# A larger first chunk in tile 0, so that its store and the load of tile 2 are issued later, in a streaming SiLU-multiply kernel

## The chip, the cores and the metric

The kernel runs on one core of a Trainium2 chip. The metric is the time of one execution in microseconds of the device. I quote medians of the fast runs, with the granted clock at 1.00. "Span" is the length of the one profiled execution; it is some 2 us shorter than the device time of the same execution.

## The reference

```python
# x: float32, (32, 512, 2048), random normal
x1, x2 = x[..., :1024], x[..., 1024:]
out = x1 * (1 / (1 + np.exp(-x1))) * x2        # float32, (32, 512, 1024)
```

134.2 MB are read and 67.1 MB written, 201.3 MB in all. There is one activation (SiLU) and one multiply for each output element.

## The kernel before

The 16,384 rows are cut into 16 tiles of 128 partitions x 8 rows. There are two input buffers and two output buffers. Loads are issued on ScalarE's DMA queue and stores on SyncE's. Each tile is computed in four chunks of 2 rows, SiLU on ScalarE and then the multiply on VectorE. After the last chunk the whole tile (4 MB) is stored, and the load of the tile after next (8 MB) is issued. Only the last tile is stored chunk by chunk.

```python
    K = 8
    KC = 2
    PLAN = [K] * (num_rows // (P * K))
    in_pool = ctx.enter_context(tc.tile_pool(name="in_pool", bufs=2))
    out_pool = ctx.enter_context(tc.tile_pool(name="out_pool", bufs=2))
    # ... cut: plan, view(), the first load moved ahead of the start barrier ...
    def load(i):
        xt = in_pool.tile([P, K, in_cols], dt, name="xt")
        nc.scalar.dma_start(out=xt[:, :plan[i][1], :], in_=view(x_flat, i))
        loaded[i] = xt

    load(0)
    load(1)
    for i in range(n_tiles):
        # ... cut: k, xt, last, ov ...
        ot = out_pool.tile([P, K, half], dt, name="ot")
        for c in range(0, k, KC):
            ce = min(c + KC, k)
            nc.scalar.activation(out=ot[:, c:ce, :], in_=xt[:, c:ce, :half],
                                 func=mybir.ActivationFunctionType.Silu)
            nc.vector.tensor_mul(out=ot[:, c:ce, :], in0=ot[:, c:ce, :],
                                 in1=xt[:, c:ce, half:])
            if last:
                nc.sync.dma_start(out=ov[:, c:ce, :], in_=ot[:, c:ce, :])
        if not last:
            nc.sync.dma_start(out=ov, in_=ot[:, :k, :])
        if i + 2 < n_tiles:
            load(i + 2)
```

## Time and profile before

| | before |
|---|---|
| median, first 3 runs | 470.96 us (470.91 to 471.08) |
| span of the profiled run | 468.9 us |
| VectorE / ScalarE busy | 30% / 25% |
| rate over the span | 429 GB/s |

These are lines of the page of the kernel before: its span, the busy tenths of the DMA engines in 40 equal slices, the chain that ended last, and the DMA issues with their time to landing.

```profile
span 468.9 us, 269 instructions
...
DMA  9899999999999998999999999999999989999998
...
DMA 80%; DVE 15%; ACT 3%; DVEq 0%; issue 0%
DMA xt<-in_x_dram 80%; DVE ot L92 15%; ACT ot L87 3%; DVEq L128 0%
...
out_dram<-ot SPq DMA_DIRECT2D x15, 4096.0 KB, 39.8
out_dram<-ot SPq DMA_DIRECT2D x4, 1024.0 KB, 5.7
xt<-in_x_dram ACTq DMA_DIRECT2D x16, 47.1
```

The DMA line has no slice under 8 tenths. The two compute engines are idle most of the time, so their work can cost time only if it leaves the DMA engines without work. The chain names VectorE for 15% of the span. That is a trap: a chain follows who released whom, and a load is released by the multiply that frees its buffer. Whether the engines stood empty meanwhile is another question, and the DMA line says no.

These are the groups of instructions of the kernel before (busy us, then the mean ns of one, then idle time and who ended it).

```profile
L92 DVE TENSOR_TENSOR ot<-ot,xt 128x2048 f32<-128x2048 f32 x64 | 142.3, 2286 | 319.5 <-ACT ot L87 319.5
L87 ACT ACTIVATE ot<-xt 128x2048 f32<-128x2048 f32 x64 | 116.9, 1897 | 338.8 <-DMA xt<-in_x_dram 338.8
```

This is the timeline of the kernel before around tiles 0 and 1 (start us, duration us, engine, line, operation, count). A row of a queue, SPq or ACTq, is the issuing of a DMA, not its transfer; the first SPq row merges four issues.

```profile
21.88 7.31 ACT L87 ACTIVATE ot<-xt 128x2048 f32<-128x2048 f32 x4 [19.31 <-DMA xt<-in_x_dram]
23.82 8.90 DVE L92 TENSOR_TENSOR ot<-ot,xt 128x2048 f32<-128x2048 f32 x4 [23.82 <-ACT ot L87]
32.74 81.08 SPq L100 DMA_DIRECT2D out_dram<-ot  x4
32.75 0.35 ACTq L74 DMA_DIRECT2D xt<-in_x_dram  x1
44.54 7.31 ACT L87 ACTIVATE ot<-xt 128x2048 f32<-128x2048 f32 x4 [15.36 <-DMA xt<-in_x_dram]
...
55.41 0.37 ACTq L74 DMA_DIRECT2D xt<-in_x_dram  x1
```

Store 0 and load 2 are issued at 32.7 us, load 1 lands at 44.5 us. And this is its end:

```profile
451.03 7.31 ACT L87 ACTIVATE ot<-xt 128x2048 f32<-128x2048 f32 x4 [21.57 <-DMA xt<-in_x_dram]
452.97 8.90 DVE L92 TENSOR_TENSOR ot<-ot,xt 128x2048 f32<-128x2048 f32 x4 [19.98 <-ACT ot L87]
455.29 6.94 SPq L98 DMA_DIRECT2D out_dram<-ot  x4
```

The trace also holds one record for every DMA packet: queue, size, start, duration. I summed them over steps of 5 us. These are not lines of a view, but my own sums for the kernel before, in GB/s:

```
  from us   loads  stores    sum      (counted from the first load packet, at 1.14 us of the span)
        0     363       0    363
        5     434       0    434
      ...
       30     424       0    424
       35     261     105    366
       40     224     210    433
      ...     the sum is 431 to 434 in every step up to 450
      450       0     434    434
      455       0     428    428
      460       0     428    428
      465       0      79     79      (the last packet ends)
```

But for the start, one dip at 35 to 40 us and the last stores, all 16 engines work at their full rate throughout. 201.3 MB at 434 GB/s is 464 us of the 468.9 us span. This agrees with the Trainium skill, "DMA: Bandwidth & Descriptors", section "Where 436 GB/s comes from", which gives a ceiling of 435.2 GB/s.

The packets of one engine show the rest. I followed each engine by joining the end of a packet to the start of the next (the records carry no engine number). The packet times here and below are counted from a zero that lies 0.13 us before that of the timelines: take 0.13 us off to compare the two. This is one of the 16 chains, L for a 64 KB load packet, s for a 32 KB store packet, as start+duration in us:

```
before, one engine:  L33.39+2.44 L35.83+3.18 s39.01+1.21 L40.22+2.42 s42.63+1.21 s43.85+1.21 L45.06+2.42 s47.47+1.21
```

A load packet takes 2.42 us and a store packet 1.21 us, in turn, for the rest of the run. Where two stores follow each other, as at 42.63 us, a 4-byte record of the load queue takes the turn between them: each DMA ends with one such record on every engine, and below an engine has "finished" a load when this record has gone out. One packet is long: the load packet just ahead of the first store packet took 3.18 us. It was so on all 16 engines, 0.87 us lost on average (0.76 to 1.00), and it does not come again. I call it the entry round.

### The profile page before, as it was taken

How to read it: one execution, taken by the hardware profiler on the slowest of the kernel's cores; microseconds unless marked ns; L12 is line 12 of the kernel's file. 1: busy time of each engine (PE TensorE's matmuls, PEld its weight loads, DVE VectorE, ACT ScalarE, POOL GpSimd, SP SyncE). 2: the span in 40 equal slices, each digit the busy share in tenths (PEclk: the TensorE clock that was granted, in tenths of full speed). 3: DMA queues.
4: the chain of work that ended last, by engine and by line, in shares of the span. 5: the costliest groups of instructions: out<-in, count | busy, mean ns of one | idle time of the engine just before them, and what ended most of it. 6: DMA issues, size and time to landing. Idle time of an engine off the chain costs nothing.

```text
span 468.9 us, 269 instructions
## 1 busy us (share of the span) xinstructions
DVE 142.3 (30%) x64; ACT 118.2 (25%) x65; POOL 0.2 (0%) x4
## 2 busy tenths in 40 slices
DVE  0070705106061160601507025070250702407034
ACT  1142406023060330603206032060420604106051
POOL 0000000000000000000000000000000000000000
DMA  9899999999999998999999999999999989999998
GB/s 431 375 447 403 447 447 447 403 419 431 447 447 403 447 492 363 442 492 391 458 403 439 456 447 403 409 442 447 447 403 444 467 386 447 442 419 481 400 409 354
DMA packets 5042, 201.35 MB, mean 429 GB/s; under 512 B 560, under 2 KB 560, under 8 KB 560
## 3 DMA queue, kind: packets, MB, share of 16 engines
q10 hardware_dynamic: 2304, 134.22, 66.4%
q1 hardware_dynamic: 2736, 67.11, 33.2%
q14 instruction: 2, 0.02, 0.0%
HBM read 134.22 MB, written 67.11 MB: 429 GB/s over the span
## 4 chain that ended last, share of the span: by engine, by line
DMA 80%; DVE 15%; ACT 3%; DVEq 0%; issue 0%
DMA xt<-in_x_dram 80%; DVE ot L92 15%; ACT ot L87 3%; DVEq L128 0%
## 5 line engine op out<-in xcount | busy, mean ns | idle before, releaser
L92 DVE TENSOR_TENSOR ot<-ot,xt 128x2048 f32<-128x2048 f32 x64 | 142.3, 2286 | 319.5 <-ACT ot L87 319.5
L87 ACT ACTIVATE ot<-xt 128x2048 f32<-128x2048 f32 x64 | 116.9, 1897 | 338.8 <-DMA xt<-in_x_dram 338.8
L87 ACT ACT_TABLE_LOAD x1 | 1.3, 1283 | 1.3 <-PEq L117 1.3
L117 POOL MEMSET const-uint8-127<- 128x1 uint8 x1 | 0.1, 102 | 0.0
L117 POOL MEMSET const-bfloat16-1.0<- 128x1 bf16 x1 | 0.1, 101 | 0.0
L117 POOL MEMSET const-float32-0.0<- 128x1 f32 x1 | 0.1, 98 | 0.2 <-issue 0.2
L117 POOL MEMSET const-float32-1.0<- 128x1 f32 x1 | 0.1, 98 | 0.0
## 6 DMA issues: line engine op xcount, KB each, us to landing
out_dram<-ot SPq DMA_DIRECT2D x15, 4096.0 KB, 39.8
out_dram<-ot SPq DMA_DIRECT2D x4, 1024.0 KB, 5.7
xt<-in_x_dram ACTq DMA_DIRECT2D x16, 47.1
```

Source lines behind the costliest of these rows:

```text
L87: nc.scalar.activation(out=ot[:, c:ce, :], in_=xt[:, c:ce, :half], func=mybir.ActivationFunctionType.Silu,)
L92: nc.vector.tensor_mul(out=ot[:, c:ce, :], in0=ot[:, c:ce, :], in1=xt[:, c:ce, half:],)
L117: nc = _bacc.Bacc("TRN2", target_bir_lowering=False, num_devices=1)
```

## The change

Its intent is to shift the moment at which the first store and the third load meet the load in flight, by giving tile 0 one large chunk first.

```diff
+    CHUNKS_FIRST = [4, 2, 2]
...
-        for c in range(0, k, KC):
-            ce = min(c + KC, k)
+        c = 0
+        for kc in CHUNKS_FIRST if i == 0 else [KC] * (k // KC):
+            ce = c + kc
             nc.scalar.activation(
...
+            c = ce
         if not last:
```

No DMA is added, removed or reordered.

## The prediction

> **What bounds the kernel.** The 16 DMA engines, from the first microsecond to the last. The page's slices show DMA at 0.9 or more in 39 of 40 slices, while DVE is busy 30% and ACT 25%. I summed the trace's packet records over 5 us steps: 434 GB/s in every step from 5 us on but for two losses. The first-load packets take 3.0 to 3.4 us instead of 2.42 us (about 0.8 us lost). The load packets that start at 35.8 us, just after the first store is issued, take 3.2 to 3.4 us instead of 2.42 us (about 0.85 us lost, once, on all 16 engines). 201.3 MB at 434 GB/s is 464 us of the 468.9 us span. The rate agrees with the 435 GB/s ceiling in the Trainium skill, "DMA: Bandwidth & Descriptors", section "Where 436 GB/s comes from".
>
> The chain of waits (DMA 80%, DVE 15%) names a load, then ACT 1.9 us, then four multiplies, then the next load. Its DVE part is no lost time: load i+1 and older stores keep the engines full meanwhile.
>
> **What the change does.** Bytes, buffers, DMA count and DMA order are unchanged. In tile 0 alone two 128x2048 pairs become one 128x4096 pair. One 128x2048 activation takes 1.89 us and one multiply 2.28 us (groups of instructions). With the small fixed part of each paid once, I estimate 3.6 us and 4.4 us for the large ones. The first multiply starts at 25.5 us instead of 23.8 us, and tile 0 ends at about 34.5 us instead of 32.7 us. Store 0 and load 2 are issued some 1.7 us later.
>
> **How much is on the critical path.** Almost none. At 34.5 us load 1 still has two or three 64 KB packets for every engine, so no engine runs dry. The packets alternate afterwards, one load of 2.42 us and one store of 1.21 us (the skill, same page, section "Queues, rings and completion order", says that engines go round-robin between queues by packet; this trace agrees). The new issue time lies close to a packet boundary (35.8 to 36.15 us). Either the store still goes in at 39 us and nothing shifts, or it goes in one load packet later, about 41.4 us. Then load 1 lands about 1.2 us earlier (43.3 instead of 44.5 us), each later tile starts about 1.2 us earlier, and that much more store backlog is left at the end. Load 15 then lands at about 449.8 instead of 451.0 us, followed by about 19 instead of 17.8 us of stores. The end is the same, since bytes and rate are. The last store chunk, issued at 461.9 us, started only at 464.5 us, so the tail has slack.
>
> **Prediction.** 470.9 us, range 470.1 to 472.0 us. Faster by over 2%: 0.01; within 2%: 0.97; slower by over 2%: 0.02.
>
> **What would show it.** Right: tile 0 has a 3.6 us activation and a 4.4 us multiply, its store is issued at 34.5 us, DMA stays full in every slice, one slow round of load packets remains, and the span is within 1 us. Wrong: a slice with a DMA gap near 35 to 45 us, packets longer than 2.42 / 1.21 us afterwards, or ACT waiting for a store instead of a load.
>
> **What would make it wrong.** If the store enters at different rounds on different engines, reads and writes would mix in time; now all engines change together within 0.4 us. Should mixed packets be slower, the whole run slows. Or the one-time loss of 0.85 us vanishes or doubles.

## The result, and the profile after

| | before | after |
|---|---|---|
| median | 471.02 us (470.71 to 471.44, 6 runs) | 471.44 us (471.0 to 471.99, 6 runs) |
| ratio of fast runs, 95% interval | | 1.0009 (0.9997 to 1.0022) |
| span of the profiled run | 468.9 us | 469.9 us |

A ratio is the mean time of one kernel's fast runs over that of the other's of the same rounds, so it is not quite the ratio of the medians. The range, 470.1 to 472.0 us, holds the median.

These are the same lines of the page, now of the changed kernel:

```profile
span 469.9 us, 267 instructions
...
DMA  9899999999999999999999999999999999999987
...
DMA 80%; DVE 15%; ACT 3%; DVEq 0%; issue 0%
DMA xt<-in_x_dram 80%; DVE ot L94 15%; ACT ot L89 3%; DVEq L131 0%
...
out_dram<-ot SPq DMA_DIRECT2D x15, 4096.0 KB, 41.3
out_dram<-ot SPq DMA_DIRECT2D x4, 1024.0 KB, 5.9
xt<-in_x_dram ACTq DMA_DIRECT2D x16, 47.1
```

No gap opened in the DMA line (its last slice, where the stores run out, reads 7 instead of 8), and the chain has the same shares. Stores take 41.3 us to land instead of 39.8 us. These are its groups of instructions, which hold 62 small and one large instruction each:

```profile
L94 DVE TENSOR_TENSOR ot<-ot,xt 128x2048 f32<-128x2048 f32 (+1 forms) x63 | 142.3, 2320 | 320.4 <-ACT ot L89 320.4
L89 ACT ACTIVATE ot<-xt 128x2048 f32<-128x2048 f32 (+1 forms) x63 | 116.9, 1925 | 339.7 <-DMA xt<-in_x_dram 339.7
```

Busy time is what it was. The durations by tile give 3.62 us for the large activation and 4.43 us for the large multiply (3.6 and 4.4 us were estimated). This is the changed kernel's timeline at the start and at the end:

```profile
21.87 7.22 ACT L89 ACTIVATE ot<-xt 128x4096 f32<-128x4096 f32 x3 [19.29 <-DMA xt<-in_x_dram]
25.52 8.83 DVE L94 TENSOR_TENSOR ot<-ot,xt 128x4096 f32<-128x4096 f32 x3 [25.52 <-ACT ot L89]
34.38 51.68 SPq L103 DMA_DIRECT2D out_dram<-ot  x3
34.38 0.35 ACTq L75 DMA_DIRECT2D xt<-in_x_dram  x1
45.85 7.31 ACT L89 ACTIVATE ot<-xt 128x2048 f32<-128x2048 f32 x4 [16.76 <-DMA xt<-in_x_dram]
...
56.73 0.37 ACTq L75 DMA_DIRECT2D xt<-in_x_dram  x1
```

```profile
451.85 7.31 ACT L89 ACTIVATE ot<-xt 128x2048 f32<-128x2048 f32 x4 [21.68 <-DMA xt<-in_x_dram]
453.80 8.89 DVE L94 TENSOR_TENSOR ot<-ot,xt 128x2048 f32<-128x2048 f32 x4 [20.09 <-ACT ot L89]
456.12 6.94 SPq L100 DMA_DIRECT2D out_dram<-ot  x4
```

The issue comes 1.64 us later (34.38 instead of 32.74 us), as forecast. But load 1 lands at 45.8 us, 1.3 us later than before, where I had expected it earlier or unchanged. The packets say why (my own chains again):

```
after, one of 15 engines:   L33.43+2.43 L35.86+2.42 L38.28+3.41 s41.68+1.21 s42.90+1.21 L44.11+2.42
after, the 16th engine:     L33.67+2.42 L36.09+2.94 s39.02+1.21 L40.23+4.18 s44.41+1.21 s45.63+1.21 L46.84+2.42
```

On 15 engines the store entered one load packet later than before, at 41.7 to 42.2 us, and the packet ahead of it lost 1.0 to 1.6 us instead of 0.87 us. The 16th engine took the store a round earlier, at 39.0 us, and then lost again, 2.29 us in all. It finished load 1 at 45.6 us, the others between 42.9 and 43.5 us. (In every later load, up to load 15, the last engine's record comes 2.4 us after the median one.) The skill, "DMA: Bandwidth & Descriptors", section "Why a DMA increments its semaphore by 16 and not by 1", says that the engines of a DMA finish independently and that only the full count of 16 means that all data has landed. This trace agrees: ScalarE started tile 1 at 45.85 us, after the sixteenth. From there on all packets last 2.42 or 1.21 us again but for isolated losses of about 0.3 us on single engines, which the kernel before has too. The last packets of 14 engines end between 467.2 and 467.8 us, the last of all at 468.7 us.

### The profile page after: what moved, and what is told of

It reads as the page before. It is cut to its first block, busy times and chain, and to the rows that moved or that the text cites. A ratio compares the mean times of both kernels' runs of the same rounds, so it can differ in the third digit from the quotient of the medians.

```text
span 469.9 us, 267 instructions
## 1 busy us (share of the span) xinstructions
DVE 142.3 (30%) x63; ACT 118.1 (25%) x64; POOL 0.2 (0%) x4
## 3 DMA queue, kind: packets, MB, share of 16 engines
q1 hardware_dynamic: 2736, 67.11, 33.1%
## 4 chain that ended last, share of the span: by engine, by line
DMA 80%; DVE 15%; ACT 3%; DVEq 0%; issue 0%
DMA xt<-in_x_dram 80%; DVE ot L94 15%; ACT ot L89 3%; DVEq L131 0%
## 5 line engine op out<-in xcount | busy, mean ns | idle before, releaser
L94 DVE TENSOR_TENSOR ot<-ot,xt 128x2048 f32<-128x2048 f32 (+1 forms) x63 | 142.3, 2320 | 320.4 <-ACT ot L89 320.4
L89 ACT ACTIVATE ot<-xt 128x2048 f32<-128x2048 f32 (+1 forms) x63 | 116.9, 1925 | 339.7 <-DMA xt<-in_x_dram 339.7
## 6 DMA issues: line engine op xcount, KB each, us to landing
out_dram<-ot SPq DMA_DIRECT2D x15, 4096.0 KB, 41.3
```

## The experiments

The theories of the first question, whether the delay costs time:

- A: the delay is absorbed, because load 1 still has packets queued; time is lost only where an engine has nothing to do.
- B: the chain of waits is the cost, so 1.6 us of delay cost 1.6 us.
- C: it is the larger instructions that matter, not the delay.

The second question is where the last +0.4 us come from: from the entry round (G), or from noise (N).

### after_again: the changed kernel on the chip of the next three runs

No edit. 

> The changed kernel once more, on the same chip as the next three runs. Theory A (the delay is absorbed by the queued packets of load 1; what is left of the difference is the dead time of the slowest of the 16 DMA engines in the one slow round of packets when the store queue starts): 0 to +1.0 us against the kernel before, and the run differs from it by what its slowest engine loses in that round. Rival B (the chain of waits is the cost: each us by which tile 0's store and load 2 come later is a us of the run, here 1.6 us): +1.6 us.

Measured: 471.58 us against 471.05 us before, ratio 1.0015 (1.0001 to 1.0029). In this profile no engine was a round apart (41.7 to 42.5 us), the mean loss in the entry round was 1.24 us, and the span was 469.6 us. B is refuted by the size.

### e4_delay_2: the delay of the store alone

```diff
+    spare = spare_pool.tile([P, 1, in_cols], dt, name="spare")    # set to 1.0 at the start
...
         # tile 0 keeps its four chunks of 2 rows
+        if i == 0:
+            for _ in range(2):
+                nc.vector.tensor_mul(out=ot[:, k-1:k, :650], in0=ot[:, k-1:k, :650],
+                                     in1=spare[:, :, :650])
         if not last:
             nc.sync.dma_start(out=ov, in_=ot[:, :k, :])
```

> The kernel before with all its 2-row chunks, and two short extra multiplies by one in tile 0 that delay its store and load 2 by about 1.7 us: the delay alone, without the 4-row instructions. Issue near 34.4 us as in the changed kernel. Theory A: within 1 us of the kernel before and within 0.5 us of the changed kernel, the store entering at a later round of packets, about 41.5 us. Rival B: +1.6 us. Rival C (the larger instructions themselves matter): equal to the kernel before, unlike the changed one.

Measured: 471.58 us, ratio 1.0008 (0.9995 to 1.0020), the same median as the changed kernel beside it. The store was issued at 34.67 us. One part of my plan was wrong: load 2 does not depend on these multiplies and was still issued at 32.9 us. So this run delays the store alone, and it looks like the changed kernel: mean loss 1.40 us in the entry round, two engines a round early, losing up to 2.5 us. Rival C is not needed: small chunks with a late store give the same picture in the packets. In the time this run alone decides nothing, as its interval holds both 1 and the changed kernel's 1.0009. Whether C adds anything below 0.5 us is not resolved by these runs.

### e2_one_chunk: tile 0 in one chunk, both issues 5 us later

```diff
-    CHUNKS_FIRST = [4, 2, 2]
+    CHUNKS_FIRST = [8]
```

> Tile 0 in one chunk of 8 rows: activation about 7.1 us, multiply about 8.7 us, so store 0 and load 2 are issued near 37.7 us, 5 us later than in the kernel before, while load 1 has packets until about 41 us. Theory A: between -0.5 and +1.0 us. Rival B: +5 us.

Measured: 470.97 us (470.71 to 471.11), ratio 0.9997 (0.9984 to 1.0009). The timeline of this run, at its start and at its end:

```profile
37.90 44.68 SPq L103 DMA_DIRECT2D out_dram<-ot  x3
37.91 0.36 ACTq L75 DMA_DIRECT2D xt<-in_x_dram  x1
42.20 7.31 ACT L89 ACTIVATE ot<-xt 128x2048 f32<-128x2048 f32 x4 [13.05 <-DMA xt<-in_x_dram]
```

```profile
448.82 7.31 ACT L89 ACTIVATE ot<-xt 128x2048 f32<-128x2048 f32 x4 [21.68 <-DMA xt<-in_x_dram]
```

A delay three times as long as that of the change costs nothing. Load 1 lands earlier, at 42.2 us, as no store packet has come ahead of its last one, and the last load lands at 448.8 instead of 451.0 us. The span is still 468.9 us, because the stores that were passed over have to be written at the end. An earlier landing of every load is worth nothing here. All engines entered together (41.4 to 42.0 us) with a mean loss of 0.82 us.

### e6_delay_18: meant to delay both by 18 us

The edit of e4_delay_2 with 15 multiplies of 1,024 columns. 

> The kernel before with 15 extra multiplies by one in tile 0: store 0 and load 2 are issued near 51 us, long after the last packet of load 1 (about 41 us). Theory A: the DMA engines are empty from about 41 to 52 us, and the run is 10 to 12 us longer, not 18. Rival B: +18 us. If the run is less than 8 us longer, the tail or another slack takes part of the gap, and theory A is incomplete.

Measured: 474.92 us, ratio 1.0063 (1.0031 to 1.0095), with three executions at 474.8 to 475.2 us and one at 471.1 us. The expectation was wrong on a false premise: again only the store was held back, to 51.8 us, while load 2, issued at 32.9 us, kept the engines full. In the profile one engine entered a round before the other 15 (56.6 us against 58.6 to 59.0 us) and lost 2.37 us there, the others 1.0 to 1.2 us. Its packets of the last load ended at 451.4 us, those of the others at 447.7 to 448.6 us, and one engine's last packet ended at 472.1 us, all others' at 468.2 to 468.3 us. The entry round is not the whole of that lag: in the chain of the early engine 21 later load packets, from 101 to 426 us, took 2.46 to 2.78 us and lost another 3.0 us in all, against at most 0.2 us on any other engine. Why this engine was slow is open. One engine that lags makes the whole core wait: the last tile had to wait for the buffer of store 13, which landed on this engine 4 us after the others (452.6 us), and the other engines stood empty for up to 0.9 us before the last stores. I had no profile of the execution at 471.1 us; that no engine lagged in it is a guess.

### e10_both_late_18: the mended form

```diff
+        if i == 0:
+            for _ in range(15):      # reads xt: load 2 has to wait
+                nc.vector.tensor_mul(out=spare[:, :, :1024], in0=xt[:, k-1:k, :1024],
+                                     in1=xt[:, k-1:k, half:half+1024])
+            nc.vector.tensor_scalar_mul(out=ot[:, k-1:k, :8], in0=ot[:, k-1:k, :8],
+                                        scalar1=1.0)     # writes ot: store 0 has to wait
```

> A mended form of the 18 us delay, whose first form had delayed only the store, as load 2 did not depend on the extra multiplies. Here 15 spare multiplies read tile 0's input, so that load 2 waits for them, and a tiny scaling of its output after them holds the store: both are issued near 51.5 us, while load 1's last packet ends near 41 us. Theory A: engines empty from 41 to about 52.5 us, and the run 10 to 12 us longer. Rival B: 18 us longer. If the run is under 8 us longer, theory A fails.

Measured: 483.43 us against 471.27 us, 12.2 us longer, ratio 1.027 (1.0251 to 1.0289). Both were issued at 51.7 us, 19 us late. The windows of this run around the hole (busy us of DVE, ACT and POOL, granted clock, DMA share, GB/s):

```profile
30.00:41.00 11.00, 10.79 (x9) 0.00 (x0) 0.00 (x0) 1.00 0.88 381
41.00:53.00 12.00, 10.41 (x10) 0.90 (x1) 0.00 (x0) 1.00 0.26 71
53.00:80.00 27.00, 8.90 (x4) 6.41 (x4) 0.00 (x0) 1.00 0.97 415
```

(The middle line is not quite zero, as the first packets of load 2 start just before 53 us.) By the packets every engine is empty from 40.5 to 41.1 us until 52.8 to 53.8 us, about 12 us, and about 12 us is what the run loses. At this dose the delay costs, and it costs what the engines stand empty: A holds, B (18 us) does not. No dose between 5 and 19 us was run, so where the cost begins is not measured.

### e11_load_late_2: load 2 alone 1.7 us later

```diff
+        if i == 0:
+            for _ in range(2):       # after the store's issue; reads xt only
+                nc.vector.tensor_mul(out=spare[:, :, :650], in0=xt[:, k-1:k, :650],
+                                     in1=xt[:, k-1:k, half:half+650])
         if i + 2 < n_tiles:
             load(i + 2)
```

> Load 2 alone comes 1.7 us later (two spare multiplies that read tile 0's input after the last real one); store 0 stays at 32.8 us. If the store's time of issue alone sets what the slow round costs, this equals the kernel before within 0.3 us: store packets enter at 39 us on all engines and load 1 lands near 44.5 us. If load 2's issue sets it, it looks like the changed kernel: entry near 41.5 us and +0.4 us or more.

Measured: 470.87 us against 471.27 us, ratio 0.9992 (0.9978 to 1.0005).

```profile
33.06 52.32 SPq L102 DMA_DIRECT2D out_dram<-ot  x3
34.74 0.33 ACTq L76 DMA_DIRECT2D xt<-in_x_dram  x1
45.17 7.31 ACT L89 ACTIVATE ot<-xt 128x2048 f32<-128x2048 f32 x4 [15.67 <-DMA xt<-in_x_dram]
```

The later load by itself does nothing. Entry at 39.1 to 39.9 us on all engines, mean loss 0.85 us, as in the kernel before. Of the two issues that the change moves, the store's is the one that alters the entry round.

### e7_warm_before: is the slow round the first use of the store queue?

```diff
     load(0)
     load(1)
+    warm = warm_pool.tile([P, 1, 128], dt, name="warm")
+    nc.sync.dma_start(out=warm, in_=view(x_flat, 0)[:, :1, :128])
```

> The kernel before, with one extra small load (128 x 128 elements, 64 KB) issued on the store queue at the start. It asks what makes the one slow round of load packets just ahead of the first store packets (35.8 us in the kernel before, 0.85 us lost). Theory F (first use of the queue): the slow round is gone from 35.8 us, and the run is 0.5 to 0.9 us shorter, unless the loss only moves to the small load at the start. Theory I (an idle queue that gets work again): the slow round stays at 35.8 us, as the queue has been idle for some 30 us, and the run is equal within 0.4 us or longer by the small load's 0.2 us.

Measured: 471.09 us against 471.27 us, ratio 1.0000 (0.9988 to 1.0013). The slow round stayed: load packets from 35.8 us on took 3.1 to 3.4 us, mean loss 0.84 us. So it is not the first use of the queue as such. The small DMA was a load, so a cost of the queue's first *write* is not excluded; it remains open beside "an idle queue that gets work".

### e9_store_first_chunk: tile 0 stored chunk by chunk

```diff
-            if last:
+            if last or i == 0:
                 nc.sync.dma_start(out=ov[:, c:ce, :], in_=ot[:, c:ce, :])
-        if not last:
+        if not last and i != 0:
             nc.sync.dma_start(out=ov, in_=ot[:, :k, :])
```

> The kernel before, with tile 0 stored chunk by chunk (four stores of 1 MB from about 26 us on) while load 2 is still issued at 32.7 us. If the slow round belongs to the store queue's start, it moves to the load packets that start near 28.6 or 31 us, with none at 35.8 us; if it belongs to load 2, it stays near 35.8 us. Theory A for the time: within 0.6 us of the kernel before, though the first store comes 6.6 us earlier and its landing too. Rival B (issue time is run time): about 6 us faster.

Measured: 475.0 us against 471.27 us, ratio 1.0082 (1.0068 to 1.0096): 3.7 us slower. Neither theory had this. The waits of this run (engine, what waited on what, total us, times, longest):

```profile
ACT ot L87 <- DMA xt<-in_x_dram: 296.8, 14, 24.4
ACT ot L87 <- DMA out_dram<-ot: 40.0, 1, 40.0
```

ScalarE waits 40.0 us, once, for a store. With chunks of 2 rows a store packet is 8 KB (0.31 us) instead of 32 KB, and it alternates one to one with a 64 KB load packet. In one of the 16 chains:

```
e9, one engine:  L28.58+2.42 s31.00+0.31 L31.31+2.55 s33.86+0.31 L34.16+2.45 s36.61+0.31 L36.92+2.44 s39.35+0.31
```

The skill, "DMA: Bandwidth & Descriptors", section "Queues, rings and completion order", says that an engine goes round-robin between queues at packet granularity. This trace agrees, and shows the consequence: the share of the rate follows the packet size. In my 5 us sums, from 30 to 40 us after the first packet, loads took 368 to 382 GB/s and stores 40 to 52 GB/s. Store 0 therefore landed so late that tile 2 got its output buffer only at 90.5 us, long after its load; by then both loads were done, and when the stores ran out too, all 16 engines had no packet for 2.5 to 3.1 us from 99.4 us on. The packets after this hole lost another 1.4 to 1.8 us. Together that is some 4.4 us on each engine, less 0.3 us that the earlier load packets lost less than before; the two profiled executions differ by 4.3 us (473.2 and 468.9 us), the medians by 3.7 us. Again, time is lost only where engines have nothing to do or start again. As for its first question: no load packet ahead of the first store lost more than about 0.2 us here (28.5 to 33 us), and none near 35.8 us lost 0.8 us. In the ten runs of the table below, whose first store packets are of 32 KB, that round lost 0.8 us or more on average. So the loss depends on more than the queue waking up.

### e12_one_packet, e13_third_packet: the store later by one packet, and by a third

The edit of e4_delay_2 with three multiplies of 630 columns (store at 35.4 us), or one (33.9 us); load 2 stays at 32.9 and 33.0 us.

> The kernel before with its store 0 alone delayed by one load packet, 2.4 us, to about 35.3 us (load 2 stays at 32.9 us): later than in the changed kernel. Theory G: the store meets the packets in the phase that it has in the kernel before, enters at about 41.5 us on all engines together, the load packet ahead of it loses about 0.85 us, and the run equals the kernel before within 0.3 us. If a later store simply costs more (rival L), it loses as much as the changed kernel or more: 1.2 us in that round and +0.5 us or more in the run.

Measured: 470.90 us (470.81 to 470.99) against 470.86 us, ratio 1.0000 (0.9987 to 1.0014). All engines entered together, at 41.6 to 42.3 us. The mean loss was 1.20 us, not the 0.85 us that G had said; and the run was equal all the same, which is against rival L. So a mean loss of 1.2 us, in place of 0.87 us, hardly shows in the run, though it does reach the end: the 16 engines' last packets end at 467.6 us on average, against 467.2 us in the kernel before.

> The kernel before with store 0 alone delayed by 0.8 us, to about 33.7 us, a third of a load packet. Theory G: still in the middle of a packet, so the entry stays at about 39 us on all engines, the loss is 0.85 us or less, and the run equals the kernel before within 0.3 us. Rival L: +0.2 us, half of what the changed kernel shows.

Measured: 471.10 us, ratio 1.0004 (0.9992 to 1.0017). G was wrong on the entry: ten engines entered at 39.3 to 39.8 us and six at 41.8 to 42.0 us. The mean loss was 1.37 us but evenly spread, 1.67 us at most, and the last packets of all engines ended within 1.1 us.

### after_third: a third profile of the changed kernel

No edit. 

> The changed kernel a third time, for a third profile and chip. Theory G (what is left of the difference, +0.4 to +0.5 us, comes from the round in which the store queue starts: with the store issued near 34.4 us its entry falls on a packet boundary, so that the load packet ahead of it loses 1.1 to 1.4 us on average instead of 0.85 us and single engines may be a round apart): 0.2 to 0.9 us above the kernel before, with the entry at about 41.8 us and a mean loss of 1.1 us or more. Rival N (noise between executions): equal, with no regular difference in that round.

Measured: 471.78 us against 470.86 us, ratio 1.0019 (1.0006 to 1.0031). Again one engine entered a round early (39.4 us, the others 41.7 to 42.2 us) and lost 2.41 us. Load 1 was complete at 45.7 us on it, by 43.4 us on the others. The last packet of one engine ended at 469.5 us, those of the other 15 at 468.0 to 468.1 us. Here one can see how a lagging engine reaches the others. Load 15 finished on one engine 3 us after the rest, and the last tile started late:

```profile
452.75 7.31 ACT L89 ACTIVATE ot<-xt 128x2048 f32<-128x2048 f32 x4 [21.69 <-DMA xt<-in_x_dram]
457.01 6.94 SPq L100 DMA_DIRECT2D out_dram<-ot  x4
```

The first store of this tile was issued at 457.0 us (455.3 us in the kernel before), and the other engines, which ran out of packets at 457.4 to 457.9 us, stood empty for up to 0.75 us. In the profile of the first run of the changed kernel (456.1 us) it came just in time, and no engine stood empty.

### What the entry round did in the profiled runs

These are my own figures from the packet chains. "Lost" is the time over 2.42 us of the load packets around the entry. "Early" counts engines that took the store a round before the rest.

| run | store issued | early engines | mean lost | most lost by one engine | last packet | median, and before beside it |
|---|---|---|---|---|---|---|
| before | 32.7 us | 0 | 0.87 us | 1.00 us | 467.8 us | 471.02 us |
| e11_load_late_2 | 33.1 us | 0 | 0.85 us | 1.01 us | 468.3 us | 470.87, 471.27 us |
| e7_warm_before | 33.3 us | 0 | 0.84 us | 1.01 us | 468.6 us | 471.09, 471.27 us |
| e13_third_packet | 33.9 us | 10 | 1.37 us | 1.67 us | 468.4 us | 471.10, 470.86 us |
| after | 34.4 us | 1 | 1.29 us | 2.29 us | 468.7 us | 471.44, 471.02 us |
| after_third | 34.5 us | 1 | 1.23 us | 2.41 us | 469.5 us | 471.78, 470.86 us |
| after_again | 34.6 us | 0 | 1.24 us | 1.40 us | 468.5 us | 471.58, 471.05 us |
| e4_delay_2 | 34.7 us | 2 | 1.40 us | 2.54 us | 468.8 us | 471.58, 471.05 us |
| e12_one_packet | 35.4 us | 0 | 1.20 us | 1.48 us | 468.0 us | 470.90, 470.86 us |
| e2_one_chunk | 37.9 us | 0 | 0.82 us | 1.01 us | 467.8 us | 470.97, 471.05 us |

Each row's last columns mix one profiled execution with a median over several, so only the pattern counts. With the store issued between 34.4 and 34.7 us, three of four profiles show one or two engines that take it a round early and lose over 2.2 us; those four medians are 0.4 to 0.9 us above the kernel before beside them. In the other rows no engine lost over 1.7 us, and the medians lie within 0.4 us on either side. But each row is one profile, and e6_delay_18, which is not in the table, has a lone early engine with the store issued at 51.8 us: that this happens only near 34.5 us is not shown. Single losses of 0.3 us and longer first packets of single engines also move the last packet by some tenths, as e7_warm_before shows.

## Why the prediction was right or wrong

**The bound: right.** (Two readings in it are off: the page's DMA line before has a 9 in 36 of 40 slices and an 8 in four, not "39 of 40"; and the first load packets lost 0.65 us on average, not 0.8 us.) In the 5 us sums the engines ran at 430 to 434 GB/s before and after, outside the start, the entry round and the end. Where they stood empty, about that time was lost (e10_both_late_18: 12 us empty, 12.2 us longer). The one run that was much slower with the engines fed, e6_delay_18, had one engine that lagged by some 3 to 4 us.

**The costs of the new instructions: right.** 3.62 and 4.43 us against 3.6 and 4.4 us, issue at 34.38 against 34.5 us.

**"Almost none" on the critical path: right.** A delay of 5 us cost nothing (e2_one_chunk). A delay of 19 us outlasted the packets of load 1, which end near 41 us, and cost the rest.

**The step that failed** is "Then load 1 lands about 1.2 us earlier (43.3 instead of 44.5 us), each later tile starts about 1.2 us earlier, and that much more store backlog is left at the end. Load 15 then lands at about 449.8 instead of 451.0 us". The store did go in one load packet later on 15 engines, whose part of load 1 was done by 43.5 us. But I had kept the loss of the entry round at its old size, 0.85 us, and taken all engines as one. It was 1.29 us on average and 2.29 us on the one engine that took the store a round early, and a load lands with its slowest engine: 45.8 us, and 451.85 us for load 15. Where all engines entered together the step's direction came true: in after_again, the same kernel, tile 1 started at 44.1 and tile 15 at 450.5 us, 0.4 and 0.6 us earlier than before in place of 1.2 us; in e12_one_packet at 43.8 and 450.0 us; in e2_one_chunk at 42.2 and 448.8 us. None of the three ended earlier for it, as the argument said. The forecast of the time could so hold although this step failed: it rests on bytes and rate, not on when load 1 lands.

**The named risk happened in part.** "If the store enters at different rounds on different engines" did occur, on one engine of 16. The fear that mixed reads and writes would then slow the whole run was wrong: packets lasted 2.42 and 1.21 us afterwards, and in e13_third_packet ten engines against six did no visible harm. What costs is one engine that falls behind alone.

**The small remainder.** The three comparisons of the changed kernel gave 1.0009, 1.0015 and 1.0019, and two of the three intervals exclude 1: the change costs some 0.1 to 0.2%, far under 2%. That it comes from the store's delay, and that later stores do not have it, is what the packets and medians suggest; the times do not show it, as the intervals of e4_delay_2 (0.9995 to 1.0020), e12_one_packet (0.9987 to 1.0014) and e2_one_chunk (0.9984 to 1.0009) overlap with the changed kernel's. Two things add up at the end in the profiles. The mean loss of the entry round arrives there in full: the last packets of the 16 engines end on average at 467.2 us before, at 467.6 us in after and after_again. And a lone late engine adds about 1 us to its own end (1.1 us after the mean in after, 1.4 us in after_third), but after_again had none and still was 0.5 us slower in the median, and in e7_warm_before and e11_load_late_2 one engine also ended 1.1 us after the mean. So the share of each is not proved. Why the load packet ahead of the first store is lengthened, and why by 0.85 us in some phases and 1.2 us in others, stays open.

No experiment beats the kernel before: e11_load_late_2 (0.9992) and e2_one_chunk (0.9997) are equal to it within their intervals. What is left over the 464 us of full rate is the start, the entry round and the last stores, a few microseconds in all, so the schedule had little to give.

## What to carry to other kernels

When the DMA engines are full all the time, ask of a delayed issue only whether the queue runs dry before it arrives: here 5 us of delay were free with some 8 us of packets queued, and 19 us cost the 12 us that were not covered. A chain of waits that runs through a compute engine does not say that the engine costs time. When two queues share the engines by packets, the packet size sets their shares, so cutting a store into small pieces can starve it, as it did for 3.7 us here; and a DMA lands with the slowest of its 16 engines, so look at the engines one by one when tenths of a microsecond have to be explained.

## What the Trainium skill lacked or had wrong

- "DMA: Bandwidth & Descriptors", section "Queues, rings and completion order": it has the round-robin by packet, but not what follows from it. With 64 KB load packets against 32 KB store packets the rate divided 2 to 1 (2.42 and 1.21 us in turn); against 8 KB store packets loads got 368 to 382 GB/s and stores 40 to 52 GB/s. It speaks of packets of some 9 to 17 descriptors; the records of this trace are of 65,536, 32,768 and 8,192 bytes, one contiguous run of a partition each.
- The same page has no word on what a queue that starts to work costs the one that is streaming: here the load packet ahead of the first store took 2.9 to 4.0 us instead of 2.42 us on every engine, once, where store packets were of 32 KB, and single engines lost up to 2.5 us.
- The same page, section "Where 436 GB/s comes from", says that for transfers between HBM and SBUF the HBM side (about 358 GB/s) binds. This single-core program held 434 GB/s of reads and writes for over 400 us. "HBM Reference", section "Specifications (TRN2)", is nearer: it says that a core that streams alone measures about 425 GB/s, bounded by its 16 DMA engines.
- The same page, section "Latency and other measured facts", gives about 600 ns to the first byte for DMAs issued from these two queues. The first load agrees: its issuing instruction runs from 0.13 to 0.50 us of the span, and its first packet starts 0.63 us later, at 1.14 us. What the page lacks is the wait of a DMA that is issued while another queue streams: the first store, issued at 32.74 us, starts at 38.9 us of the span at the earliest, 6.1 us later. That it stands behind load packets already taken up is my reading, not shown.
